# Second expert matrix read in 8 KB runs, and the sorted copy of the modulated rows made later by two engines

## The chip, the cores and the metric

The kernel runs on one core of one Trainium2 chip. The metric is the device time of one execution in microseconds (us). A core has a matrix engine (PE, with its weight loads as PEld), a vector engine (DVE), an activation engine (ACT), a general engine (POOL), and a queue engine (SP) that issues most of the transfers (DMA) between the main memory and the on-chip memory (SBUF). Matmuls write to a second memory, PSUM, in tiles of up to 512 columns per bank. About 0.2%, or 3.7 us, is what a measurement of this kernel can tell from no change.

## The reference

One layer on 512 tokens of width 1024, all in float32:

```python
h = modulate(rms_norm(x, g_mix[l]), sh_a, sc_a)
u = h @ w_in[l]
...
x = x + gt_a[:, None, :] * (merged @ w_o[l])
h = modulate(rms_norm(x, g_ffn[l]), sh_f, sc_f)
x = x + gt_f[:, None, :] * moe(h, w_router[l], b_router[l], w_mlp1[l], b_mlp1[l], w_mlp2[l], b_mlp2[l])
```

`merged` comes from a retention branch and from dilated attention with three head groups of four heads each; groups 1 and 2 take their keys with a stride. The second half is a mixture of 32 experts, four per token. One expert on its rows:

```python
u = xb @ w1[e] + b1[e]
glu = jnp.minimum(u[:, ::2], SWIGLU_LIMIT)
lin = jnp.clip(u[:, 1::2], -SWIGLU_LIMIT, SWIGLU_LIMIT)
a = glu * jax.nn.sigmoid(SWIGLU_ALPHA * glu) * (lin + 1.0)
return a @ w2[e] + b2[e]
```

`w1[e]` is 1024 x 2048, `w2[e]` is 1024 x 1024.

## The kernel before

**Precision.** Matmuls run on operands that are split in two parts, a rounded high part and the rest. ACT makes the high part (`w_hl` at L203 and L229, `w_hi` at L1045), DVE subtracts it from the raw tile for the low part (L204, L230, `w_lo` at L1051). DVE's instruction has both inputs in SBUF.

**Attention stage.** The modulated rows lie transposed in `hTh` and `hTl` (high and low part, 128 partitions x 8 chunks x 512 tokens). Groups 1 and 2 need the tokens sorted by their place modulo 4: ACT and DVE sort queries and keys when they copy them out of PSUM (`query`, L509; `key`, L515; group 0 unsorted at L507 and L517). For the values the rows themselves are the stationary operand, so a sorted copy `hpr` of `hTh` and `hTl` is made, 8 chunks each, by `reorder` on POOL (L438). It is read by the values of heads 1 to 3 (`unit_tok` with `hp`); head 0 reads the rows with a stride. `hpr` takes the buffer in which the bias table `pbt` lay.

For each head the order is: `scores` (PE L527 for groups 1 and 2, L535 for group 0; DVE adds the bias at L529 and L539, ACT takes the exponential at L544), a round trip of the softmax sums through main memory, issued by POOL (`st` at L545 and L546, `so` at L548 and L549), then the next head's query products, `merge` (DVE L554 to L567, which reads `so`), and `values` (transposes L584, products L595, sum L608, split L609 and L610). Then come a product for the modulation row (`ada_row_pe`, PE L273, DVE L275, store by POOL L278) and the next head's keys. `retire` splits the next weight tile whenever one has been used. In head 0 the 16 copies of `reorder` are issued between the query products. This part is in an order written by hand: each engine runs its instructions in the order of the code.

**Experts.** `tiles` lists 384 tiles of 1 MB: for each expert eight A tiles (128 rows of `w1`) and four B tiles (256 rows of `w2`), in the order A of expert e, then B of expert e - 1. Experts are sorted by load. Large ones ("L") have 96 slots and three matmul passes (high x high, low weights, low rows), small ones ("S") have 64 slots, and both parts of the rows stand side by side as one stationary operand, so two passes do. The kinds are `"LLLL" + "LS" * 14`. The tiles go through a ring of nine slots. SP loads a tile when DVE has made the low part of the tile nine places ahead; ACT works four tiles ahead of PE (`prep_hi`), DVE three (`prep_lo`). The first expert matrix comes with 2048 numbers (8 KB) per partition and tile. For the second one two rows of 1024 numbers, 128 rows apart, make up a partition's part:

```python
SP.dma_start(w.rearrange("p (k n) -> p k n", k=2),
             w2[0, at].rearrange("o (k p) n -> p (o k) n", p=P)[:, 2 * k:2 * k + 2])
```

**Around the activation.** `u` is one PSUM buffer of four banks. When an expert's A tiles are done, ACT writes the sigmoid `sg` (`open_gates`, L1200), DVE writes `av` (`linear`, L1205) and multiplies it in place (`times_glu`, L1209); these read every second column of `u`, and then the next expert's bias matmul (L1140) may write `u`. Later DVE multiplies `av` by `sg` (`times_gate`, L1212), PE transposes `av` in two halves of four chunks (`turn`, L1178), and ACT and DVE write the parts of `at` (`turn_copy`, L1122 and L1123). That is done in the A tiles 2 and 3 of the following expert, for the last expert ahead of its first B tile. B tile k then uses chunks 2k and 2k + 1 of `at` (L1369 for large, L1376 for small experts). For a large expert the sigmoid stands on ACT ahead of the last copy of the next expert's turned rows, `x`.

Of the kernel before, what the change touches and what calls it, by code (L numbers as in the profile page):

```python
# [12 lines left out]
F32R = mybir.dt.float32r  # L13
# [3 lines left out]
AF = mybir.ActivationFunctionType  # L17
# [97 lines left out]
def body(tc, a, out):  # L115
# [318 lines left out]
    def reorder(i, kcs):  # L434
        src = (hTh, hTl)[i]
        for kc in kcs:
            o, x = hp[i][:, kc].rearrange("p (t a) -> p t a", t=4), src[:, kc].bitcast(F32).rearrange("p (a t) -> p t a", t=4)
            G.tensor_copy(o, x)  # L438
    s1 = ExitStack()
    p1c = s1.enter_context(tc.tile_pool(name="p1c", bufs=1, side="right", reuse_waits="tile"))  # L440
    p1w = s1.enter_context(tc.tile_pool(name="p1w", bufs=2, side="right", reuse_waits="tile"))
# [176 lines left out]
    for h in range(4):  # L618
# [9 lines left out]
            unit_tok(parts["v0", 0], None, v0f, (0,))  # L628
            bias_flip(bf, range(4))
        s, st, so = scores(h, qT, kT)  # L630
        if h == 0:
            hpr = p2c.tile([P, 2, KC, S], F32R, name="hpr", tag="hp")
            hp = [hpr[:, 0], hpr[:, 1]]
        ada = ada_row_sum(h)
        if h == 0:
            unit_tok(parts["v0", 0], None, v0f, (1,))
# [9 lines left out]
        if h < 3:  # L646
            qT = []
            for g in range(3):
                qT.append(query(g, unit(None, hTh, hTl, parts=parts[AQ, g, h + 1])))
                retire(1)  # L650
                if h == 0:
                    for i in range(2):
                        reorder(i, range(3 * g, min(3 * g + 3, KC)))
                if g == 1:
                    merge(s, st, so)
            last = (AK, 1, h + 1)
        else:
            rq0 = unit_open("ps")
            unit_part(rq0, parts[RQ, 0], hTh, hTl, range(KC))
            merge(s, st, so)  # L660
            last = (RK, 0)
# [3 lines left out]
            kT = {1: key(1, pf)}  # L665
        retire(1)
        ada_row_pe(h, ada)
        if h < 3:
            for g in (2, 0):
                kT[g] = key(g, unit(None, hTh, hTl, parts=parts[AK, g, h + 1]))  # L670
                retire(1)
    s1.close()


# [200 lines left out]
    def load(i, pool, tag):  # L875
        kind, e, k = tiles[i]
        w = pool.tile([P, 2048], F32, name="w_moe", tag=tag)
        if kind == "A" and k == 0 and e > 1:
            which[e] = nc.values_load(sorted_i[0:1, e:e + 1], engines=[mybir.EngineType.SP], min_val=0, max_val=E - 1)
        at = ds(which[e], 1) if e > 1 else slice(e, e + 1)  # L880
        if kind == "A":
            SP.dma_start(w, w1[0, at].rearrange("o (k p) n -> p (o k) n", p=P)[:, k])
        else:
            SP.dma_start(w.rearrange("p (k n) -> p k n", k=2),
                         w2[0, at].rearrange("o (k p) n -> p (o k) n", p=P)[:, 2 * k:2 * k + 2])
        loaded[i] = w

    ring = [(wr, "wr")] * NRA + [(hl, "hl")] * NRC
# [304 lines left out]
    def fold(ps, low):  # L1193
        for j in range(ps.shape[1]):
            PE.matmul(ps[:SMALL, j], shift[SMALL:], low[SMALL:, j], start=False, stop=True, skip_group_check=True)

    def open_gates(u):
        n = u.shape[0]
        sg = m2.tile([CAP, 4, 256], F32, name="sg", bufs=1)[:n]
        A.activation(sg, u[:, :, ::2], AF.Sigmoid, scale=1.702)  # L1200
        return sg

    def linear(u):
        av = m2.tile([CAP, 4, 256], F32, name="av", bufs=1)[:u.shape[0]]
        V.tensor_scalar(av, u[:, :, 1::2], 8.0, -6.0, op0=OP.min, op1=OP.max)  # L1205
        return av

    def times_glu(u, av):
        V.scalar_tensor_tensor(av, u[:, :, ::2], 7.0, av, op0=OP.min, op1=OP.mult)  # L1209

    def times_gate(sg, av):
        V.scalar_tensor_tensor(av, sg, top7[:av.shape[0], 1:2], av, op0=OP.min, op1=OP.mult)  # L1212
# [107 lines left out]
    for i, (kind, e, k) in enumerate(tiles):  # L1320
# [33 lines left out]
        else:  # L1354
# [8 lines left out]
            if KIND[e] == "L":  # L1363
                ah, al = AT[e]
                for s_, m_ in ((ah, hi), (ah, lo), (al, hi)):
                    for c in range(2):
                        for n in range(2):
                            col = c * 1024 + n * 512
                            PE.matmul(Y[e][:CAP, n], s_[:, 2 * k + c], m_[:, col:col + 512], start=False,  # L1369
                                      stop=(k == 3 and s_ is al and c == 1))  # L1370
            else:
                for m_ in (hi, lo):
                    for c in range(2):
                        for n in range(2):
                            col = c * 1024 + n * 512
                            PE.matmul(Y[e][:, n], AT[e][2][:, 2 * k + c], m_[:, col:col + 512],  # L1376
                                      start=(k == 0 and c == 0 and m_ is hi), stop=False, skip_group_check=True)
                        if k == 0 and c == 0 and m_ is hi:
                            for n in range(2):
                                bias_mm(Y[e][:SMALL, n], e, 4 + n, False)  # L1380
# [62 lines left out]
    with tc.For_i(0, extra) as it:  # L1443
# [34 lines left out]
            PE.matmul(y[:, n], ones_r[0:1, :CAP], bb2[:, n * 512:(n + 1) * 512], start=True, stop=False)  # L1478
        for k in range(4):
            w = wc.tile([P, 2, D], F32, name="w_x2", tag="lo")  # L1480
            SP.dma_start(w, w2[0, ds(ev, 1)].rearrange("o (k p) n -> p (o k) n", p=P)[:, 2 * k:2 * k + 2])
            for c in range(2):
                for n in range(2):
                    PE.matmul(y[:, n], aT[:, 2 * k + c], w[:, c, n * 512:(n + 1) * 512], start=False,
                              stop=(k == 3 and c == 1))
        finish(y, gate_, idx)

# [50 lines left out]
```

## Time and profile before

| | us |
|---|---|
| median of 3 runs | 1853.34 (1851.53 to 1855.56) |
| the profiled execution | 1853.22 |
| its span, first to last instruction | 1851.4 |
| PE busy | 1750.5 (95%) |
| DVE busy | 1457.3 (79%) |
| ACT busy | 1094.7 (59%) |
| POOL busy | 349.7 (19%) |

The busy time is summed over the whole span, and the stages differ: up to about 620 us the projections, attention and retention, to about 720 us the output product and the router, to about 1800 us the experts, then the final norm. A row of the timeline has the start, the duration, the engine, the line, the operation, its operands (partitions x elements) and, in brackets, how long the engine was idle before and what ended that. Matmuls overlap, so the duration of one is longer than the step from one to the next.

### The profile page before, as it was taken

How to read it: one execution, taken by the hardware profiler on the slowest of the kernel's cores; microseconds unless marked ns; L12 is line 12 of the kernel's file. 1: busy time of each engine (PE TensorE's matmuls, PEld its weight loads, DVE VectorE, ACT ScalarE, POOL GpSimd, SP SyncE). 2: the span in 40 equal slices, each digit the busy share in tenths (PEclk: the TensorE clock that was granted, in tenths of full speed). 3: DMA queues.
4: the chain of work that ended last, by engine and by line, in shares of the span. 5: the costliest groups of instructions: out<-in, count | busy, mean ns of one | idle time of the engine just before them, and what ended most of it. 6: DMA issues, size and time to landing. Idle time of an engine off the chain costs nothing.

```text
span 1851.4 us, 23571 instructions
## 1 busy us (share of the span) xinstructions
PE 1750.5 (95%) x8625; PEld 1329.4 (72%) x8625; DVE 1457.3 (79%) x1490; ACT 1094.7 (59%) x1064; POOL 349.7 (19%) x220
## 2 busy tenths in 40 slices
PE   5988999999999998999999999999999999999982
PEld 4877888888778876677766776776676677677661
DVE  7555535657564558799989999999999999999994
ACT  5232233222222324677878977987887887898781
POOL 2031001100110111023631221211212112122111
PEclk8998999999999997999999999999999999999996
DMA  9523423633565555799999999999999999999993
GB/s 314 158 69 92 114 72 89 208 91 95 162 171 148 178 231 204 275 369 374 373 367 389 405 388 397 397 396 401 385 408 399 388 404 394 385 405 390 397 356 115
DMA packets 207910, 525.49 MB, mean 284 GB/s; under 512 B 12102, under 2 KB 127222, under 8 KB 174896
## 3 DMA queue, kind: packets, MB, share of 16 engines
q1 hardware_dynamic: 197744, 494.99, 71.5%
q0 software_dynamic: 10048, 28.98, 6.3%
q8 instruction: 69, 1.13, 0.3%
q14 instruction: 49, 0.40, 0.1%
HBM read 503.67 MB, written 20.25 MB: 283 GB/s over the span
## 4 chain that ended last, share of the span: by engine, by line
PE 74%; DVE 12%; DMA 7%; issue 4%; ACT 3%; SPq 0%; DVEq 0%; POOL 0%; ACTq 0%; POOLq 0%
PE u L1344 22%; DVE w_lo L1051 6%; PE pp L213 6%; PE pp L215 6%; PE pp L214 6%; PE y L1369 5%; PE u L1349 5%; PE y L1376 5%; DMA w_moe<-in_w_mlp 4%; DMA s_acc<-ys,idx 2%; PE pp L247 2%; PE pp L245 2%; PE pp L246 2%; PE pt L1178 2%; PE u L1140 2%
## 5 line engine op out<-in xcount | busy, mean ns | idle before, releaser
L1051 DVE TENSOR_TENSOR w_lo<-w_moe,w_hi 128x2048 fp32r<-128x2048 f32 x384 | 862.7, 2277 | 11.1 <-ACT w_hi L1045 5.7
L1045 ACT ACTIVATE w_hi<-w_moe 128x2048 fp32r<-128x2048 f32 x384 | 728.6, 1914 | 166.5 <-PE u L1344 103.9
L1344 PE MATMUL u<-w_hi,x 128*96 128x512 f32 x1152 | 313.2, 402 | 0.1
L1169 POOL DMA_INDIRECT xg<-s_h,idx x31 | 145.9, 4705 | 669.7 <-ACT gate L1165 345.8
L1344 PEld LDWEIGHTS u<-w_hi,x 128*96 128x96 f32 x1152 | 182.4, 163 | 75.2 <-issue 0.3
L213 PE MATMUL pp<-hTh,w_hl 128*128 128x512 f32 x400 | 160.4, 401 | 0.0
L1344 PE MATMUL u<-w_lo,x 128*96 128x512 f32 x576 | 158.8, 398 | 1.2 <-DVE w_lo L1051 1.2
L214 PE MATMUL pp<-hTl,w_hl 128*128 128x512 f32 x400 | 156.6, 391 | 0.0
L215 PE MATMUL pp<-hTh,w_hl 128*128 128x512 f32 x400 | 156.5, 391 | 0.0
L1369 PE MATMUL y<-w_hi,at 128*96 128x512 f32 x576 | 153.1, 398 | 0.0
L204 DVE TENSOR_TENSOR w_hl<-w_raw,w_hl 128x1024 fp32r<-128x1024 f32 (+1 forms) x66 | 87.5, 1338 | 76.8 <-ACT w_hl L203 76.8
L1349 PE MATMUL u<-w_lo,x 128*128 128x512 f32 x448 | 125.7, 402 | 3.7 <-DVE w_lo L1051 2.6
L1349 PE MATMUL u<-w_hi,x 128*128 128x512 f32 x448 | 128.9, 409 | 0.0
L1219 POOL DMA_INDIRECT s_acc<-ys,idx x32 | 97.3, 3040 | 164.7 <-ACT ys L1218 149.3
L1344 PEld LDWEIGHTS u<-w_lo,x 128*96 128x96 f32 x576 | 94.4, 164 | 42.8 <-DVE w_lo L1051 1.6
L1369 PEld LDWEIGHTS y<-w_hi,at 128*96 128x96 f32 x576 | 92.1, 162 | 38.7 <-issue 0.4
L203 ACT ACTIVATE w_hl<-w_raw 128x1024 fp32r<-128x1024 f32 (+1 forms) x66 | 65.2, 1001 | 70.8 <-PE pp L215 54.1
L1349 PEld LDWEIGHTS u<-w_lo,x 128*128 128x128 f32 x448 | 82.0, 188 | 34.3 <-DVE w_lo L1051 15.8
L1349 PEld LDWEIGHTS u<-w_hi,x 128*128 128x128 f32 x448 | 79.1, 188 | 19.9 <-issue 5.4
L213 PEld LDWEIGHTS pp<-hTh,w_hl 128*128 128x128 f32 x400 | 75.5, 189 | 17.9 <-issue 3.1
L215 PEld LDWEIGHTS pp<-hTh,w_hl 128*128 128x128 f32 x400 | 75.4, 188 | 16.2
L214 PEld LDWEIGHTS pp<-hTl,w_hl 128*128 128x128 f32 x400 | 75.5, 189 | 14.6
(342 smaller groups left out, 2699.2 us busy)
## 6 DMA issues: line engine op xcount, KB each, us to landing
w_moe<-in_w_mlp SPq DMA_DIRECT2D x384, 1024.0 KB, 12.9
w_raw<-in_w_in SPq DMA_DIRECT2D x76, 512.0 KB, 5.4
w_ada<-in_w_ada SPq DMA_DIRECT2D x24, 1024.0 KB, 7.1
w_raw<-in_w_ret_o SPq DMA_DIRECT2D x8, 512.0 KB, 4.7
w_o<-in_w_o SPq DMA_DIRECT2D x4, 1024.0 KB, 5.0
s_acc<-z POOLq DMA_DIRECT2D x5, 512.0 KB, 7.2
xin<-in_x SPq DMA_DIRECT2D x4, 512.0 KB, 6.6
w_raw<-in_w_att_o SPq DMA_DIRECT2D x8, 256.0 KB, 6.4
```

The source lines that it names most:

```text
L204: eng.tensor_tensor(lo[:, :kc], raw, hi[:, :kc].bitcast(F32), op=OP.subtract)
L213: PE.matmul(ps, hi[:, k], mh[:, k], start=(k == 0), stop=False)
L214: PE.matmul(ps, hi[:, k], ml[:, k], start=False, stop=False)
L215: PE.matmul(ps, lo[:, k], mh[:, k], start=False, stop=(k == kc - 1))
L1045: A.activation(his[i], loaded[i], AF.Copy)
L1051: V.tensor_tensor(los[i], loaded[i], his[i].bitcast(F32), op=OP.subtract)
L1169: G.indirect_dma_start(out=xg, out_offset=None, in_=xn2, in_offset=bass.IndirectOffsetOnAxis(ap=idx[:, :1], axis=0))
L1219: G.indirect_dma_start(out=acc, out_offset=bass.IndirectOffsetOnAxis(ap=idx[:, :1], axis=0), in_=ys, in_offset=None, compute_op=OP.add)
L1344: PE.matmul(U[e][:CAP, j], s_[:, k], m_[:, j * 512:(j + 1) * 512], start=False, stop=(k == KC - 1 and s_ is xl))
L1349: PE.matmul(U[e][:, j], X[e][2][:, k], m_[:, j * 512:(j + 1) * 512], start=(k == 0 and m_ is hi), stop=False, skip_group_check=True)
L1369: PE.matmul(Y[e][:CAP, n], s_[:, 2 * k + c], m_[:, col:col + 512], start=False, stop=(k == 3 and s_ is al and c == 1))
L1376: PE.matmul(Y[e][:, n], AT[e][2][:, 2 * k + c], m_[:, col:col + 512], start=(k == 0 and c == 0 and m_ is hi), stop=False, skip_group_check ...
```

## The change

For the second expert matrix each partition reads 2048 consecutive numbers, that is rows 2p and 2p + 1 of a tile's 256, where it read rows p and p + 128. The stationary chunks must hold the same rows: chunk 4c + k has to hold the rows 256k + 2p + c. This order is made when `sg` and `av` are written: `by_row` is the sorted view of an SBUF tile, `pairs` the view of `u` that goes with it. Element 2m + c is written to place 512c + m.

The sorted copy of the modulated rows is made after head 0's `values` and the modulation row: the low part by POOL in eight copies, the high part by ACT in two groups of four among the next head's key products.

```diff
+            if i:
+                G.tensor_copy(o, x)
+            else:
+                A.activation(o, x, AF.Copy)
...
-                if h == 0:
-                    for i in range(2):
-                        reorder(i, range(3 * g, min(3 * g + 3, KC)))
...
         ada_row_pe(h, ada)
+        if h == 0:
+            hpr = p2c.tile([P, 2, KC, S], F32R, name="hpr", tag="hp")
+            hp = [hpr[:, 0], hpr[:, 1]]
+            reorder(1, range(KC))
         if h < 3:
-            for g in (2, 0):
+            for i, g in enumerate((2, 0)):
                 kT[g] = key(g, unit(None, hTh, hTl, parts=parts[AK, g, h + 1]))
                 retire(1)
+                if h == 0:
+                    reorder(0, range(4 * i, 4 * i + 4))
...
-            SP.dma_start(w.rearrange("p (k n) -> p k n", k=2),
-                         w2[0, at].rearrange("o (k p) n -> p (o k) n", p=P)[:, 2 * k:2 * k + 2])
+            SP.dma_start(w, w2[0, at].rearrange("o (k p c) n -> p (o k) (c n)", p=P, c=2)[:, k])
...
+    def by_row(t):
+        return t.rearrange("p j i -> p (j i)").rearrange("p (c m) -> p m c", c=2)
+
+    def pairs(u, i):
+        return u.rearrange("p j i -> p (j i)")[:, i::2].rearrange("p (m c) -> p m c", c=2)
+
-        A.activation(sg, u[:, :, ::2], AF.Sigmoid, scale=1.702)
+        A.activation(by_row(sg), pairs(u, 0), AF.Sigmoid, scale=1.702)
...
-        V.tensor_scalar(av, u[:, :, 1::2], 8.0, -6.0, op0=OP.min, op1=OP.max)
+        V.tensor_scalar(by_row(av), pairs(u, 1), 8.0, -6.0, op0=OP.min, op1=OP.max)
...
-        V.scalar_tensor_tensor(av, u[:, :, ::2], 7.0, av, op0=OP.min, op1=OP.mult)
+        V.scalar_tensor_tensor(by_row(av), pairs(u, 0), 7.0, by_row(av), op0=OP.min, op1=OP.mult)
...
-                            PE.matmul(Y[e][:CAP, n], s_[:, 2 * k + c], m_[:, col:col + 512], start=False,
+                            PE.matmul(Y[e][:CAP, n], s_[:, 4 * c + k], m_[:, col:col + 512], start=False,
```

The same new index stands in the small experts' matmul, and the new load and index in the loop for overflowing experts.

On POOL, from head 0's stores of the softmax sums to those of head 1, before the change (L438 is `reorder`, L259 and L278 load and store the modulation row, L522 clears a part of `s` for the next `scores`):

```order
L545 DMA s_sta<-st 128x4x2
L546 DMA s_stb<-st 128x8
L548 DMA so<-s_stb 128x4x2
L549 DMA so<-s_sta 128x8
L259 DMA brow<-in_b_ada 1x16x16
L438 CAST hpr<-hTh 128x512 x3
L438 CAST hpr<-hTl 128x512 x3
...
L278 DMA s_mod<-brow 16x1x16
L522 MEMSET s 128x128
```

And after it (line numbers of the changed kernel):

```order
L548 DMA s_sta<-st 128x4x2
L549 DMA s_stb<-st 128x8
L551 DMA so<-s_stb 128x4x2
L552 DMA so<-s_sta 128x8
L259 DMA brow<-in_b_ada 1x16x16
L278 DMA s_mod<-brow 16x1x16
L439 CAST hpr<-hTl 128x512 x8
L525 MEMSET s 128x128
```

The copies went from the place ahead of the store of the modulation row to the place behind it, and eight of the sixteen left this engine.

On ACT, the end of head 0's `values` to the exponentials of head 1, after the change (L441 is `reorder`, L203 and L229 are the high parts of weight tiles, L612 is the high part of the attention output, L547 the exponential, L590 and L610 copy out of PSUM):

```order
L590 ACTIVATE pT<-pt 128x384
L610 ACTIVATE ao<-po 128x512
L612 ACTIVATE atH<-ao 128x512
L229 ACTIVATE w_hl<-w_raw 128x4x128 x4
L203 ACTIVATE w_hl<-w_raw 128x1024
L441 ACTIVATE hpr<-hTh 128x512 x4
L203 ACTIVATE w_hl<-w_raw 128x1024
L441 ACTIVATE hpr<-hTh 128x512 x4
L547 ACTIVATE s,st<-s,st 128x256 x8
```

Before the change the two splits L203 stood next to each other, and there were no copies into `hpr` on ACT.

On DVE, around the activation of a large expert in the changed kernel (L1053 is `w_lo`, L1125 the low part of turned rows, L1213 `linear`, L1217 `times_glu`, L1220 `times_gate`):

```order
L1053 TENSOR_TENSOR w_lo<-w_moe,w_hi 128x2048
L1125 TENSOR_TENSOR x<-pt,x 128x4x64
L1053 TENSOR_TENSOR w_lo<-w_moe,w_hi 128x2048
L1213 TENSOR_SCALAR av<-u 96x512x2
L1217 SCALAR_TENSOR_TENSOR av<-u,av 96x512x2
L1053 TENSOR_TENSOR w_lo<-w_moe,w_hi 128x2048 x2
```

The order is that of before; the two `av` instructions have the form 96x512x2 where they had 96x1024.

## Rows read from the trace of the kernel before

**Rows 1.** Busy time by stage; columns: stretch, length, PE, PEld, DVE, ACT, POOL, clock, DMA.

```profile
1000.00:1250.00 250.00, 248.60 (x1183) 176.09 (x1181) 240.07 (x150) 206.91 (x165) 52.75 (x15) 1.00 1.02 395
```

**Rows 2.** Chain of waits through one pair of experts; columns: start, length, what.

```profile
1000.20 5.54 PE u L1344 x24
...
1046.80 0.04 DVEq L1051
...
1064.16 1.23 DVE av L1209
...
1065.53 1.13 PE u L1140 x4
```

**Rows 3.** Timeline of another pair, ACT and DVE around the activation.

```profile
1224.14 1.02 ACT L1200 ACTIVATE sg<-u 96x1024 f32<-96x1024 f32 x1 [1.39 <-PE u L1344]
1225.07 0.37 ACT L1122 ACTIVATE x<-pt 128x256 fp32r<-128x256 f32 x1
1225.47 0.43 DVE L1123 TENSOR_TENSOR x<-pt,x 128x256 fp32r<-128x256 f32 x1 [2.48 <-ACT x L1122]
...
1263.65 1.22 DVE L1209 SCALAR_TENSOR_TENSOR av<-u,av 64x1024 f32<-64x1024 f32 x1
```

**Rows 4.** Waits in 1000 to 1750 us; columns: total us, times, longest.

```profile
ACT w_hi L1045 <- DMA w_moe<-in_w_mlp: 8.2, 16, 1.7
```

**Rows 5.** Waits of the queue engine in 1000 to 1750 us.

```profile
SPq L882 <- DVE w_lo L1051: 267.4, 149, 3.0
```

**Rows 6.** Instructions by form in 1000 to 1750 us; after the bar: busy us, mean ns.

```profile
L1209 DVE SCALAR_TENSOR_TENSOR av<-u,av 96x1024 f32<-96x1024 f32 x11 | 13.4, 1221 | 0.4
L1205 DVE TENSOR_SCALAR av<-u 96x1024 f32<-96x1024 f32 x11 | 13.4, 1214 | 0.0
...
L1200 ACT ACTIVATE sg<-u 96x1024 f32<-96x1024 f32 x11 | 11.2, 1021 | 15.1 <-PE u L1344 15.1
```

**Rows 7.** DVE by form in 80 to 330 us: a sum in steps, a difference in plain order.

```profile
L608 DVE TENSOR_TENSOR ao<-ao,po 128x512 f32<-128x512 f32 x4 | 4.4, 1091 | 19.8 <-PE po L595 19.8
...
L610 DVE TENSOR_TENSOR atL<-ao,atH 128x512 fp32r<-128x512 f32 x4 | 2.8, 692 | 2.8 <-ACT atH L609 2.8
```

**Rows 8.** DVE by form in 560 to 760 us: copies that write in a row, in steps.

```profile
L945 DVE CAST selb<-sel 128x128 bf16<-128x128 f32 x4 | 0.9, 228 | 0.1
...
L963 DVE CAST aux<-rg 128x120 bf16<-128x120 f32 x1 | 0.4, 439 | 0.0
```

**Rows 9.** Timeline of head 0 for POOL, DVE and PE, engine by engine.

```profile
125.96 3.15 POOL L438 CAST hpr<-hTh 128x512 fp32r<-128x512 f32 x3
...
140.39 2.10 POOL L438 CAST hpr<-hTl 128x512 fp32r<-128x512 f32 x2
...
130.09 13.48 DVE L204 TENSOR_TENSOR w_hl<-w_raw,w_hl 128x1024 fp32r<-128x1024 f32 x1 [4.21 <-ACT w_hl L203]
...
133.53 0.39 PE L215 MATMUL pp<-hTh,w_hl 128*128 128x512 f32 x1
145.54 1.17 PE L584 MATMUL pt<-misc,s 128*128 128x128 f32 x4 [11.62 <-DVE s L567]
```

**Rows 10.** Chain of waits, heads 0 and 1: first transposes and modulation product.

```profile
157.76 0.52 PE pb L273 x2
...
200.58 0.44 PE pt L584 x4
...
211.14 0.52 PE pb L273 x2
```

**Rows 11.** Timeline behind head 0's values for POOL, DVE and PE, engine by engine.

```profile
164.46 0.22 POOL L522 MEMSET s<- 128x128 f32 x1
...
165.10 1.23 DVE L204 TENSOR_TENSOR w_hl<-w_raw,w_hl 128x1024 fp32r<-128x1024 f32 x1 [0.41 <-ACT w_hl L203]
...
169.45 0.69 DVE L517 COPY k<-pp 128x512 f32<-128x512 f32 x1 [3.12 <-PE pp L215]
...
171.04 1.69 PE L535 MATMUL sc<-k,q 128*128 128x128 f32 x8
```

More of the change, by code (lines that the diff above doesn't have):

```diff
@@ L437, in reorder @@
             o, x = hp[i][:, kc].rearrange("p (t a) -> p t a", t=4), src[:, kc].bitcast(F32).rearrange("p (a t) -> p t a", t=4)
-            G.tensor_copy(o, x)
+            if i:
+                G.tensor_copy(o, x)
+            else:
+                A.activation(o, x, AF.Copy)
     s1 = ExitStack()
@@ L630, in body @@
         s, st, so = scores(h, qT, kT)
-        if h == 0:
-            hpr = p2c.tile([P, 2, KC, S], F32R, name="hpr", tag="hp")
-            hp = [hpr[:, 0], hpr[:, 1]]
         ada = ada_row_sum(h)
@@ L650, in body @@
                 retire(1)
-                if h == 0:
-                    for i in range(2):
-                        reorder(i, range(3 * g, min(3 * g + 3, KC)))
                 if g == 1:
@@ L1375, in body @@
                             col = c * 1024 + n * 512
-                            PE.matmul(Y[e][:, n], AT[e][2][:, 2 * k + c], m_[:, col:col + 512],
+                            PE.matmul(Y[e][:, n], AT[e][2][:, 4 * c + k], m_[:, col:col + 512],
                                       start=(k == 0 and c == 0 and m_ is hi), stop=False, skip_group_check=True)
@@ L1480, in body @@
             w = wc.tile([P, 2, D], F32, name="w_x2", tag="lo")
-            SP.dma_start(w, w2[0, ds(ev, 1)].rearrange("o (k p) n -> p (o k) n", p=P)[:, 2 * k:2 * k + 2])
+            SP.dma_start(w, w2[0, ds(ev, 1)].rearrange("o (k p c) n -> p (o k) c n", p=P, c=2)[:, k])
             for c in range(2):
                 for n in range(2):
-                    PE.matmul(y[:, n], aT[:, 2 * k + c], w[:, c, n * 512:(n + 1) * 512], start=False,
+                    PE.matmul(y[:, n], aT[:, 4 * c + k], w[:, c, n * 512:(n + 1) * 512], start=False,
                               stop=(k == 3 and c == 1))
```

## The prediction

> **What bounds the kernel now.** I read the table by stage first, then the chain of waits inside one stage, then the waits, and last the single rows. From about 740 us to 1800 us the kernel streams 32 experts, and there all three resources are nearly full: in 1000 to 1250 us PE is busy 248.60 of 250 us, DVE 240.07, and the DMA engines read 1.02 [rows 1]. Such shares name no bound, so the chain decides. The experts come as four large ones (L, three matmul passes) and then 14 pairs of a large and a small one (S, two passes). One pair is 66.4 us: the chain enters the A tiles of a large expert at 1000.20 and the next large one's bias matmul at 1065.53 [rows 2]. Up to 1046.80 the chain is PE's; from there it is DVE's, ending with `linear` (L1205) and `times_glu` (L1209), which read the one PSUM buffer `u` and so free it for PE's next bias matmul (L1140). PE starts 0.14 us after L1209's end at 1065.39.
>
> The stretch of PE and that of DVE are tied together. When PE ends the A tiles of a large expert, ACT makes the sigmoid (L1200, 1224.14), then copies the transposed rows of the next expert (1225.07), and DVE, idle for 2.48 us, goes on at 1225.47 [rows 3]. From there DVE has no gap of this kind until L1209 at 1263.65 has freed `u` for the next large expert, at 1264.87. In that run lie both L1205/L1209 couples of the pair, the large expert's early and the small one's at the end. So a pair is: PE's A tiles of the large expert (about 25 us), the ACT sigmoid and one copy (1.4 us), then 39.4 us of DVE. Whatever is added to one of the four DVE instructions, or to the large expert's sigmoid, is added to the pair.
>
> DMA has no such place. SP issues its loads when DVE has released a slot (267.4 us of waits behind `w_lo` in 750 us) [rows 5], and ACT, which uses the tiles first, waited for a load only 8.2 us in 750, 16 times [rows 4]. ACT is idle at other times, and PE and DVE were not found waiting behind these.
>
> Earlier there is one large hole: in head 0 PE is idle 11.62 us before the transposes at 145.54 [rows 9]. DVE is the cause, and POOL behind it: the split of a weight tile (L204) that begins at 130.09 lasts 13.48 us, where its like lasts 1.23, and POOL makes its 16 copies into `hpr` from 125.96 to 142.49. L204 has two SBUF inputs; it ended at 143.57, 1.08 us after POOL's last copy. `merge` stands behind it on DVE, and its last step lets PE go on.
>
> **The change part by part.** *Loads in runs of 8 KB.* The same 1 MB per tile, the same queue and slots, 128 loads in the other shape. The 8.2 us in 750, some 11 in the 1050 us of this stage, bound what it can give, and nothing on the chain waits for it: I take 0, between a gain of 11 us and nothing. If this cover went, ACT would wait for tiles, and `w_lo` behind it.
>
> *PE's side.* Chunk 4c + k of `at` in place of 2k + c. Both halves of the turned rows are made in the A tiles of the following expert, ahead of the B tiles, and for the last expert both before its first B tile: no new wait, 0.
>
> *The price of the other row order.* Rows 2p and 2p+1 of a run of 8 KB lie in one partition, so the activations must be sorted, and the change does it where they are written: `sg` and `av` are written with neighbours 512 elements (2 KB) apart, and `times_glu` also reads `av` so. Counts per expert: one ACT instruction (L1200, now 1.02 us) and two DVE instructions (L1205 1.21, L1209 1.22) [rows 6]. At 1024 elements these run at about one element per cycle now, so a gain is excluded. What a jump at each element costs, no row shows for this distance. Nearest is L608, which reads and writes SBUF in steps of four elements, in place, as L1209 will: 1.091 us against 0.692 for L610 of the same size with plain rows, so 0.40 us per 512 elements [rows 7], 0.80 per 1024. L1209 is of this kind: 0.80. L1205 only writes in jumps: between 0 and 0.80. That a stepping write alone costs is seen in L963, 439 ns for 120 elements written in steps, against 228 for 128 in a row [rows 8]; that is 1.76 ns per element and 1.8 us per 1024, the upper end for either instruction. I take 0.70 for L1205, near L608. For ACT no row has an SBUF operand in steps; between 0 and 0.80, I take 0.40.
>
> The Trainium skill (Vector Engine (DVE) Microarchitecture Reference, "Measured stream behaviour on trn2") says that a DVE port runs at full rate only when consecutive elements come in adjacent pairs, and gives 1.71 ns per column for a destination that hops 4 KiB at every element and 1.98 with all streams hopping, against 1.054. As an estimate from that page L1205 would take 0.67 us more and L1209 0.95, and the forecast would be 3 us higher. No run here shows it at 2 KB.
>
> The sum for this part: per pair 2 x (0.70 + 0.80) + 0.40 = 3.4 us; the small expert's sigmoid isn't on the run. 14 pairs give 47.6 us. In the first four experts, all large, PE has 12 matmuls per tile of 0.231 us (5.54 us for 24 [rows 2]), 2.77 us against a small expert's 1.85, for the same work of DVE; there PE is the longer one, and I count nothing.
>
> *The sorted copy moved.* Removed: POOL's 16 copies in head 0, so L204 takes its 1.23 us and ends near 131.3; the load of `so` that `merge` reads is issued by POOL ahead of the first copy, 5 us before; from L204's end to the transposes it takes 2.0 us (143.57 to 145.54), so they are due near 133.3, when PE is still at its last matmuls (the last starts at 133.53). The 11.62 us go. With them goes PE's slow start behind the hole: from the transposes to the `ada` product 145.54 to 157.76 is 12.22 us in head 0, 200.58 to 211.14 is 10.56 in head 1 [rows 10], 1.66 us more. Gain: 13.28 us.
>
> Added: POOL makes eight copies behind the store of the `ada` row of head 0. Today a memset of `s` stands there at 164.46 [rows 11]; the copies take half of 16.53 us, so till 172.73 (times before the shift). DVE's next L204 comes at 165.10 and waits as the one in head 0 did, to 1.08 us after POOL: 173.81. Behind it stands the copy of the first group's keys (L517), from 169.45 to 170.14 today, then to 174.50; PE's scores of that group (L535) started at 171.04 and wait till 174.55. That is 3.5 us of PE, plus between 0 and 1.66 for a slow start behind a shorter hole, I take 0.5. Behind the copies on POOL stand the memset and, later, the stores of `st`; DVE writes `s` only from about 175.7, behind another split of 1.23 us, so the memset is in time. ACT's eight copies, each between 0.51 (half of L1200) [rows 6] and POOL's 1.05 [rows 9], go four behind the split of which L204 at 165.10 is DVE's half, and four behind the next one at 169.45: done by 174.8 at the latest, and the product that reads `hpr` now starts near 176. Net gain of this part: 13.28 - 3.5 - 0.5 = 9.3 us.
>
> The Trainium skill (SBUF — State Buffer, "Who interferes with whom") says that DVE with two SBUF inputs and a reading POOL instruction exclude each other for the length of one instruction, whoever starts first. By that L204 would get in after one copy (1.05 us), L517 would not be late, the 3.5 us would not arise and the forecast would be 4 us lower; the row of 13.48 us, behind twelve copies, speaks against it.
>
> **Forecast.** The profiled execution took 1853.2 us (span 1851.4 and 1.8 around it), the median of the three runs is 1853.3, so nothing has to be scaled. 1853.2 - 9.3 + 47.6 = 1891.5 us.
>
> **The rivals.** *Jumps of 2 KB cost DVE and ACT nothing.* For it: L1205 and L1209 read PSUM in steps of two today at one element per cycle [rows 6], so steps alone need not cost. Against it: L608 and L963. Then the part in the experts is 0 and the time 1843.9, faster. It decides from 9.3 / 14 = 0.66 us per pair, about 0.16 us for each of the four DVE instructions: below that the kernel is not slower. *They cost a part*, only one of the two instructions or a third of L608's price: 14 x 0.5 to 14 x 1.7, so 1851 to 1868. *They cost as in L963*, 1.8 us each on DVE and ACT: 14 x (4 x 1.8 + 1.8) = 126, so 1970. *The loads of 8 KB pay*: the 11 us of waits come back, 1880; inside the range. *POOL lets DVE in between two copies*: L204 waits one copy of 1.05 us at most, PE's 4.0 us are not lost, 1887.5; against it stands L204's 13.48 us, so 0.1 of the forecast's chance.
>
> **How the numbers follow.** Forecast, with the terms of L1205 between 0.4 and 0.8, L1209 between 0.6 and 1.0 and ACT between 0 and 0.8, 1872 to 1905: chance 0.70. Free: 0.15. A part: 0.09. As L963 or in between: 0.06. The range 1850 to 1920 leaves out the free case and the dearest one. About 0.2%, 3.7 us, is what a measurement of this kernel can tell from no change. Faster by more: 0.16, nearly all from the free case; within: 0.03; slower: 0.81.
>
> **What would show it.** Right: `av` on DVE near 1.9 and 2.0 us in place of 1.21 and 1.22, a pair of experts near 69.8 us in place of 66.4, PE waiting at L1140 for `av`, and ACT's waits for loads gone without effect; in head 0 no L204 of 13 us and no hole before the transposes, and in head 1 one L204 of about 8.7 us with PE waiting some 3.5 us before L535. Wrong: `av` at 1.2 us, or `av` longer and the pair still 66.4 us (then DVE had slack that I don't see), or a changed rate of the loads that moves the pair.

## The result, and the profile after

| | before | after |
|---|---|---|
| median, four runs each on the same chip, us | 1853.19 (1851.53 to 1855.56) | 1912.69 (1910.41 to 1913.47) |
| after over before, 95% interval | | 1.0317 (1.0303 to 1.0330) |
| span of the profiled execution, us | 1851.4 | 1910.3 |

The change makes the kernel 59.5 us slower; the forecast was 38.3 us slower. The sign was right, and so was the mechanism in the stage of the experts; the size was too small by 21 us.

The stage of the experts comes first. Its busy times by stretch, in the order of [rows 1]:

```profile
1000.00:1250.00 250.00, 238.79 (x1104) 164.09 (x1104) 233.02 (x141) 196.09 (x153) 82.23 (x14) 0.99 0.98 372
```

PE was busy 248.60 of 250 us and is now busy 238.79. DVE didn't fill the place: it went from 240.07 to 233.02, because fewer experts pass in the same time. So PE waits, and the chain of waits shows for what. This is one pair of experts, to be read against [rows 2] (start, length, what):

```profile
1000.17 1.14 PE u L1142 x4
1001.31 5.55 PE u L1352 x24
...
1030.68 1.96 DVE av L1213
1032.65 2.15 DVE av L1217
1034.94 1.17 PE u L1357 x4
...
1066.67 1.96 DVE av L1213
1068.66 2.07 DVE av L1217
1070.86 1.99 PE u L1142 x4
```

The pair takes 70.69 us (1000.17 to 1070.86), where it took 66.47 (999.06 to 1065.53). Both couples of `linear` (L1213) and `times_glu` (L1217) now lie on the chain, with 1.96 to 2.15 us each. The two forms of each in 1000 to 1750 us (behind the bar busy us and mean ns), to be read against [rows 6]:

```profile
L1217 DVE SCALAR_TENSOR_TENSOR av<-u,av 96x1024 f32<-96x1024 f32 x11 | 23.5, 2140 | 0.4
L1217 DVE SCALAR_TENSOR_TENSOR av<-u,av 64x1024 f32<-64x1024 f32 x11 | 22.8, 2069 | 0.4
L1213 DVE TENSOR_SCALAR av<-u 96x1024 f32<-96x1024 f32 x11 | 22.3, 2029 | 0.0
L1208 ACT ACTIVATE sg<-u 96x1024 f32<-96x1024 f32 x11 | 22.3, 2025 | 15.1 <-PE u L1352 15.1
```

`linear` went from 1.21 to 2.03 us, `times_glu` from 1.22 to 2.10 (mean of the two forms), the sigmoid of the large experts from 1.02 to 2.03. The waits in the same 750 us (total us, times, longest):

```profile
PE u L1142 <- DVE av L1217: 21.8, 11, 2.0
PE u L1357 <- DVE av L1217: 7.1, 10, 0.7
```

PE waits 2.0 us for `av` ahead of each large expert and 0.7 ahead of each small one. Before, PE was idle for 0.26 us at that place in the pair of [rows 2].

Attention is the other place. POOL, DVE and PE around heads 0 and 1, against [rows 9] and [rows 11]:

```profile
149.89 8.43 POOL L439 CAST hpr<-hTl 128x512 fp32r<-128x512 f32 x8
...
128.84 1.23 DVE L204 TENSOR_TENSOR w_hl<-w_raw,w_hl 128x1024 fp32r<-128x1024 f32 x1 [4.21 <-ACT w_hl L203]
150.53 8.87 DVE L204 TENSOR_TENSOR w_hl<-w_raw,w_hl 128x1024 fp32r<-128x1024 f32 x1 [0.40 <-ACT w_hl L203]
...
132.50 0.60 PE L587 MATMUL pt<-misc,s 128*128 128x128 f32 x4
...
160.15 3.32 PE L538 MATMUL sc<-k,q 128*128 128x128 f32 x8 [3.52 <-DVE k L520]
```

The split at 128.84 takes 1.23 us and the transposes follow at 132.50 without a hole. In head 1 the split at 150.53 waits behind POOL's eight copies and takes 8.87 us, and PE waits 3.52 us for the key copy behind it.

The 58.9 us between the two spans, cut at the bias matmul on `u` of the experts named (from the timeline):

| stretch | before | after | difference |
|---|---|---|---|
| start to expert 0 | 710.47 | 702.63 | -7.84 |
| expert 0 to 4 | 152.77 | 156.35 | +3.58 |
| 4 to 5 | 38.12 | 38.02 | -0.10 |
| the 13 steps from a small to a large expert | 413.16 | 451.58 | +38.42 |
| the 13 steps from a large to a small one | 453.87 | 476.30 | +22.43 |
| expert 31 to the end | 83.01 | 85.42 | +2.41 |

### The profile page after: what moved, and what is told of

It is laid out like the page before. It is cut to its first block, busy times and chain, and to the rows that moved or that the text cites. A ratio compares the mean times of both kernels' runs of the same rounds, so it can differ in the third digit from the quotient of the medians.

```text
span 1910.3 us, 23571 instructions
## 1 busy us (share of the span) xinstructions
PE 1775.6 (93%) x8625; PEld 1326.6 (69%) x8625; DVE 1503.5 (79%) x1490; ACT 1132.9 (59%) x1072; POOL 457.5 (24%) x212
## 2 busy tenths in 40 slices
DMA packets 191526, 525.49 MB, mean 275 GB/s; under 512 B 12102, under 2 KB 127222, under 8 KB 142128
## 4 chain that ended last, share of the span: by engine, by line
PE 65%; DVE 27%; issue 4%; DMA 2%; ACT 1%; DVEq 0%; SPq 0%; POOL 0%; POOLq 0%; ACTq 0%
PE u L1352 22%; DVE w_lo L1053 16%; PE pp L213 6%; PE pp L215 6%; PE pp L214 6%; PE u L1357 5%; DVE av L1217 3%; DVE av L1213 3%; PE y L1377 2%; PE pp L247 2%; PE pp L245 2%; PE pp L246 2%; PE u L1142 2%; PE pt L1180 1%; PE y L1384 1%
## 5 line engine op out<-in xcount | busy, mean ns | idle before, releaser
L1053 DVE TENSOR_TENSOR w_lo<-w_moe,w_hi 128x2048 fp32r<-128x2048 f32 x384 | 862.2, 2277 | 5.7 <-issue 2.7
L1227 POOL DMA_INDIRECT s_acc<-ys,idx x32 | 303.1, 9473 | 233.8 <-ACT ys L1226 217.8
L1352 PE MATMUL u<-w_hi,x 128*96 128x512 f32 x1152 | 318.6, 407 | 0.0
L1171 POOL DMA_INDIRECT xg<-s_h,idx x31 | 57.6, 1858 | 546.8 <-PE y L1384 264.0
L204 DVE TENSOR_TENSOR w_hl<-w_raw,w_hl 128x1024 fp32r<-128x1024 f32 (+1 forms) x66 | 82.9, 1268 | 78.0 <-ACT w_hl L203 78.0
L1357 PE MATMUL u<-w_lo,x 128*128 128x512 f32 x448 | 130.8, 413 | 11.9 <-DVE w_lo L1053 10.2
L1357 PEld LDWEIGHTS u<-w_lo,x 128*128 128x128 f32 x448 | 77.3, 188 | 60.2 <-DVE w_lo L1053 46.7
L203 ACT ACTIVATE w_hl<-w_raw 128x1024 fp32r<-128x1024 f32 (+1 forms) x66 | 65.2, 1002 | 66.7 <-PE pp L215 45.2
```

What stands on the lines that cost most here:

```text
L203: A.activation(hi[:, :kc], raw, AF.Copy)
L204: eng.tensor_tensor(lo[:, :kc], raw, hi[:, :kc].bitcast(F32), op=OP.subtract)
L1053: V.tensor_tensor(los[i], loaded[i], his[i].bitcast(F32), op=OP.subtract)
L1171: G.indirect_dma_start(out=xg, out_offset=None, in_=xn2, in_offset=bass.IndirectOffsetOnAxis(ap=idx[:, :1], axis=0))
L1227: G.indirect_dma_start(out=acc, out_offset=bass.IndirectOffsetOnAxis(ap=idx[:, :1], axis=0), in_=ys, in_offset=None, compute_op=OP.add)
L1352: PE.matmul(U[e][:CAP, j], s_[:, k], m_[:, j * 512:(j + 1) * 512], start=False, stop=(k == KC - 1 and s_ is xl))
```

## The experiments

Each run was timed beside the kernel before on its own chip, which gave medians of 1852.8 to 1853.4 us.

**The two parts apart.** The second part alone takes over the new `reorder` and its calls and leaves loads and activations as before:

```diff
-                if h == 0:
-                    for i in range(2):
-                        reorder(i, range(3 * g, min(3 * g + 3, KC)))
...
+            reorder(1, range(KC))
...
+                    reorder(0, range(4 * i, 4 * i + 4))
```

> The kernel before with the second part alone: the sorted copy moved behind head 0's values and shared by POOL and ACT; loads and activations as before. Theory of the prediction: the hole of 11.62 us in head 0 and the slow start behind it go, and 3.5 to 4 us come back as a wait of the group-0 scores in head 1, so 9.3 us less than before, 1844. The trace of the changed kernel stands 7.8 us ahead at the first expert, of which 1.3 us lie ahead of the first instruction, so 1844 to 1847. Rival: the time of the attention stage is taken up again by a wait for loads at the start of the experts, then 1853.

Measured: 1843.43 us, ratio 0.9952 (0.9935 to 0.9968), 9.9 us less. The first part alone, with the loads, the index and the sorted writes:

> The kernel before with the first part alone: loads of 8 KB runs, activations written sorted, the sorted copy of the rows where it was. Theory: the two parts add up, so the changed kernel's 1912.7 plus the 7 to 9 us that the other part gives: 1920 to 1922. The step from a small to a large expert is 3.3 us longer than before, and from a large to a small one 0.9 or 2.5 us. Rival: part of the loss is a collision of the two parts (an earlier start that the loads then have to catch up with), then 1910 to 1914.

Measured: 1922.03 us, ratio 1.0363 (1.0345 to 1.0380), 68.7 us more. The parts add up: 68.7 - 9.9 = 58.8, and the change gave 59.5. The rival of a collision falls. (In the profiled executions a lower clock behind a wait, told below, came in nine places with the first part alone and in seven with the whole change, 3.2 us apart; closer than that the sum can't be read.)

**What the loads are worth.** The loads and the index, with plain `sg` and `av`:

```diff
+            SP.dma_start(w, w2[0, at].rearrange("o (k p c) n -> p (o k) (c n)", p=P, c=2)[:, k])
...
+                            PE.matmul(Y[e][:CAP, n], s_[:, 4 * c + k], m_[:, col:col + 512], start=False,
```

> The kernel before with the loads of 8 KB runs and the new chunk index, and no sorting anywhere: the activations are left in plain order, so they meet the wrong rows of the second expert matrix; the work is otherwise that of before. It shows what the loads alone are worth. In the kernel with the sort at the transposes ACT waited for loads 3.8 us in the experts against 8.2, and none of the steps from a small to a large expert was longer than 31.75 us, where before three of thirteen were, by 3.8 us together. Theory: the loads give 3 to 5 us, 1849. Rival A, as predicted: 0, 1853. Rival B: they give the 11 us, 1842.

Measured: 1853.09 us, ratio 1.0000 (0.9990 to 1.0010). My theory here fell and the prediction's zero stands. ACT's waits for loads between 740 and 1770 us are

```profile
ACT w_hi L1044 <- DMA w_moe<-in_w_mlp: 8.2, 11, 2.1
```

and the kernel before has 8.2 us too, in 16 waits. The late steps that I had put down to the short runs occur here as well: 32.02, 32.44 and 35.74 us where 31.65 is the rule. They come at partly other experts in each run, and the loads' shape doesn't decide on them.

What makes such a step long shows in the chain of the kernel before, here through its step of 32.77 us (start, length, what):

```profile
1437.80 13.90 DMA w_moe<-in_w_mlp
...
1451.81 1.92 ACT w_hi L1045
1453.73 0.03 issue
1453.76 1.88 ACT low L1190
...
1455.68 1.14 PE u L1195 x4
```

`low` (L1190) is ACT's copy of the part of a small expert's products that PE then adds to the rest (L1195). In this step ACT waited 1.71 us for a tile, where in a step of 31.64 us (expert 19) it waited 0.46 for the tile of the same place; so `low` came late and PE waited 1.48 us for it. PE waits for `low` in four places between 740 and 1770 us in the kernel before, 3.7 us in total, and in four with the loads in the new shape, 4.0 us. So loads do reach the chain in a few places, which the prediction had left out, and longer runs don't cure it.

**Where the sort is made: on PE.** The activations are written in plain order, and the transposes read every second column:

```diff
+            part = rows[:, 2 * P * i + q:2 * P * (i + 1):2] if by_two else rows[:, c * P:(c + 1) * P]
+            PE.transpose(pt[:, i, :n], part, ident[:n, :n])
```

> The kernel before with the loads of 8 KB runs and the new index of the chunks, but the activations written in plain order; the sort is made where PE transposes them: each transpose reads 128 of 256 columns with step 2. The sorted copy of the rows stays where it was. Theory (the jumping writes alone cost the time): L1205 and L1209 are back at 1.21 us, the sigmoid at 1.02, a pair at 66.4 us, the time 1853, between 1850 (if the longer runs of the loads give a little) and 1856 (if PE pays for the stepping read of its stationary operand, 16 transposes per expert). Rival A: the loads of 8 KB themselves hold up the pair, then over 1870 with av at 1.21 us. Rival B: the loads pay by the 11 us of waits that ACT has for them: 1842.

Measured: 1859.04 us, ratio 1.0031 (1.0021 to 1.0040), 5.7 us more; `av` is back at 1.21 us. Rival A falls with it: the loads don't hold up the pair. The 5.7 us are PE's. The weight load of one transpose of a small expert's `av` in 1000 to 1750 us, first before, then here:

```profile
L1178 PEld LDWEIGHTS pt<-misc,av 64*128 64x128 f32 x96 | 7.8, 139 | 9.3 <-issue 8.9 <-DVE w_lo L1051 0.4
```

```profile
L1178 PEld LDWEIGHTS pt<-misc,av 64*128 64x128 f32 x92 | 12.7, 208 | 8.9 <-issue 8.9
```

That is 69 ns for each of eight transposes, 0.55 us. They lie in the A tiles of the large expert that follows, where PE is on the chain, and the step from a large to a small expert grew from 34.83 to 35.28. The transposes of a large expert's `av` lie in the other step and need as much more (207 ns against 141), but that step stayed at 31.65: DVE has no gap there. 13 x 0.45 = 5.9 us. Other steps of the two profiled executions differ too, by up to 2.7 us, some up and some down, so the match with 5.7 is not as close as it looks.

**Where the sort is made: while reading PSUM.** The same sorted `sg` and `av`, but the instructions walk through the SBUF tile in order and through `u` in steps of four. Only the order of the dimensions in the two views differs from the change:

```diff
-        return t.rearrange("p j i -> p (j i)").rearrange("p (c m) -> p m c", c=2)
+        return t.rearrange("p j i -> p (j i)").rearrange("p (c m) -> p c m", c=2)
...
-        return u.rearrange("p j i -> p (j i)")[:, i::2].rearrange("p (m c) -> p m c", c=2)
+        return u.rearrange("p j i -> p (j i)")[:, i::2].rearrange("p (m c) -> p c m", c=2)
```

> The kernel before with the loads of 8 KB runs, the new chunk index and the sorted sg and av, but each of the three instructions walks through the sorted tile in order and steps through u instead: SBUF written and read in plain rows, PSUM read in steps of four elements instead of two. Theory (jumps on the SBUF side cost, steps in PSUM don't): L1205 and L1209 at 1.21, the sigmoid at 1.02 us, and the time of the kernel with the loads alone, 1849 to 1851. Rival: a step of four in PSUM costs like one in SBUF, 0.8 us per 1024 elements: then the time of the first part alone, 1915 to 1922.

Measured: 1853.57 us, ratio 1.0001 (0.9991 to 1.0011). The three instructions in 1000 to 1750 us:

```profile
L1214 DVE SCALAR_TENSOR_TENSOR av<-u,av 96x1024 f32<-96x1024 f32 x11 | 13.4, 1220 | 0.4
L1210 DVE TENSOR_SCALAR av<-u 96x1024 f32<-96x1024 f32 x11 | 13.4, 1214 | 0.0
...
L1205 ACT ACTIVATE sg<-u 96x1024 f32<-96x1024 f32 x11 | 11.2, 1021 | 15.2 <-PE u L1349 15.2
```

They take as long as before. So the whole price of the first part is the jump on the SBUF side, and it was not needed: the same order of values comes at no cost from the step in PSUM.

The trace of the kernel before had this to show already. In attention, ACT's copies of queries at L509 and DVE's of keys at L515 sort while they step through PSUM by four elements and write SBUF in a row; L507 and L517 copy without sorting (80 to 330 us):

```profile
L507 ACT ACTIVATE q<-pp 128x512 f32<-128x512 f32 x6 | 3.6, 595 | 15.7 <-PE pp L215 15.7
L509 ACT ACTIVATE q<-pp 128x512 f32<-128x512 f32 x3 | 1.8, 599 | 7.5 <-PE pp L215 7.5
...
L517 DVE COPY k<-pp 128x512 f32<-128x512 f32 x3 | 2.1, 692 | 11.0 <-PE pp L215 11.0
L515 DVE COPY k<-pp 128x512 f32<-128x512 f32 x6 | 4.1, 687 | 1.0 <-PE pp L215 1.0
```

The sort costs neither engine anything there, so the cheap order of the dimensions could have been chosen from the trace.

**DVE's share and ACT's share.** Sorted writes for the sigmoid alone, and for `av` alone, each with the new loads:

```diff
-        A.activation(sg, u[:, :, ::2], AF.Sigmoid, scale=1.702)
+        A.activation(by_row(sg), pairs(u, 0), AF.Sigmoid, scale=1.702)
```

> The kernel before with the loads of 8 KB runs and the new index, where only the sigmoid sg is written in jumps and av in plain order: the two factors don't match then, so the activation is computed in part wrongly; the work is the same. Theory: the sigmoid is 1.0 us longer, that of the large expert lies in the pair's run, and the step from a large to a small expert grows by 0.95 us, fourteen times, 13 us over the kernel with the loads alone: 1862 to 1863. The step from a small to a large one stays at 31.65. Rival: the 0.95 us belongs to DVE's longer instructions, and ACT has room for its longer one: 1849 to 1850.

```diff
-        V.tensor_scalar(av, u[:, :, 1::2], 8.0, -6.0, op0=OP.min, op1=OP.max)
+        V.tensor_scalar(by_row(av), pairs(u, 1), 8.0, -6.0, op0=OP.min, op1=OP.max)
...
-        V.scalar_tensor_tensor(av, u[:, :, ::2], 7.0, av, op0=OP.min, op1=OP.mult)
+        V.scalar_tensor_tensor(by_row(av), pairs(u, 0), 7.0, by_row(av), op0=OP.min, op1=OP.mult)
```

> The first part of the change with av written in jumps (both DVE instructions) and the sigmoid sg in plain order: the two factors don't match then, so the activation is computed in part wrongly; the work is the same. The counterpart of the kernel with the jumping sigmoid alone, which is 7.5 us slower than before with 0.95 us more per pair. Theory (the terms of a pair add up): 2 x (0.82 + 0.89) = 3.4 us per pair, 48 us, plus up to eight steps that are 1.6 us longer by the lower clock, so 1901 to 1914, and a pair 0.95 us shorter than in the first part alone. Rival: the longer sigmoid hides behind the longer DVE instructions, then 1922 like the first part alone.

Measured: 1860.76 us (ratio 1.0046, 1.0029 to 1.0063) and 1908.73 us (1.0298, 1.0281 to 1.0315). The steps between the bias matmuls of experts 8 (large), 9 (small) and 10 (large), from the timelines:

| kernel | 8 to 9 | 9 to 10 | the pair |
|---|---|---|---|
| before | 34.83 | 31.64 | 66.47 |
| sigmoid in jumps | 34.86 | 32.61 | 67.47 |
| `av` in jumps | 34.84 | 34.93 | 69.77 |
| both (the changed kernel) | 35.78 | 34.91 | 70.69 |
| both (the first part alone) | 37.36 | 34.94 | 72.30 |

The sigmoid adds 1.00 us to a pair, `av` 3.30, both 4.22: the terms add, as the sum in the prediction had it. The sigmoid shows in the second step where it jumps alone, and in the first where `av` jumps as well. My expectation had the wrong step; I take it to be a matter of where PE meets the wait, which no run tests. Where only `av` jumps, nine of the thirteen steps from a large to a small expert are 1.6 us longer (36.45), of which the next experiment tells more. The sigmoid's share of the total is only 7.5 us. Twelve of the 13 steps from small to large are 0.96 us longer, 11.5 us, but their sum grew by 7.6 (413.16 to 420.75). Before, three of them were longer than their like (32.77, 33.72 and 32.24 against 31.64), 3.8 us together, and here none is. These are steps with the waits for `low` told above; in that of 33.72 us the granted clock also fell behind the wait of 0.88 us (0.74 in 1525 to 1530 us). With the sigmoid in jumps ACT waits for no load between 740 and 1770 us, nor does it in the changed kernel, and in none of these steps does PE wait for `low`. So a slower pair leaves the late loads more time, and part of its price comes back.

**The lower clock behind the wait.** In the table the first part alone has a step of 37.36 where the changed kernel has 35.78. Both values occur in both kernels: in the changed one, from expert 6 on, seven of the thirteen such steps take about 37.36 us and six 35.8 (the expectation below says eight, which is one too many). Ten matmuls that nobody reads were put in the place of the wait:

```diff
+                    if e and KIND[e - 1] == "S":
+                        warm = psC.tile([P, 4, CAP], F32, name="warm", tag="pt", bufs=2)
+                        for _ in range(10):
+                            PE.matmul(warm[:CAP].rearrange("p a b -> p (a b)"), sel[:, 0, e:e + 1].to_broadcast([P, CAP]),
+                                      btile[:, :4 * CAP], start=True, stop=True)
```

> The changed kernel with ten matmuls of 384 columns, whose result nobody reads, ahead of the bias matmul of each large expert that follows a small one, where PE waits some 2 us for av. In the changed kernel eight of the steps from a large to a small expert are 37.36 us and six 35.8; in the long ones the granted clock is 0.68 to 0.72 in the 5 us behind the wait. Theory: the wait lets the clock fall, and work in its place keeps it up; all steps become 35.8, 8 x 1.6 = 12.7 us less than the changed kernel, 1900. Rival: the long steps have another cause (the bias matmul itself, or the load of its weights), then 1912 to 1913, or more if the added matmuls run into the bias matmul's time.

Measured: 1899.88 us, ratio to before 1.0254 (1.0237 to 1.0271), 12.8 us less than the changed kernel. All thirteen steps are 35.77 to 35.83 us. In the changed kernel, the 5 us behind the bias matmul of experts 10 and 12, with the granted clock in the last but two column:

```profile
1071.00:1076.00 5.00, 5.00 (x16) 3.38 (x17) 5.00 (x3) 0.85 (x1) 3.87 (x1) 0.68 1.02 351
1143.30:1148.30 5.00, 5.00 (x22) 3.46 (x22) 5.00 (x3) 1.99 (x2) 3.94 (x1) 1.00 1.03 342
```

Both came behind a wait of 2.0 us, and PE began 16 matmuls in the one stretch and 22 in the other; 0.68 is a mix of the two levels, 1.2 and 2.4 GHz. With the matmuls in the wait:

```profile
1067.58 1.89 PE L1349 MATMUL warm<-btile,selrow 128*96 128x384 f32 x10
...
1069.80 1.13 PE L1142 MATMUL u<-btile,selrow 128*96 128x512 f32 x4 [0.33 <-DVE av L1217]
```

```profile
1069.80:1074.80 5.00, 5.00 (x22) 3.55 (x23) 5.00 (x3) 1.97 (x2) 3.83 (x1) 1.00 1.03 341
```

The matmuls fill 1.89 of the 2 us, the steps to a large expert stay within 0.1 us of what they were, and the clock stays up. So about 11 us (7 x 1.58), of the 59.5, are a second price of the wait.

**No copy on POOL.** To test whether DVE waits for POOL's copies at all, all sixteen were given to ACT, in the order of before otherwise:

```diff
-            G.tensor_copy(o, x)
+            A.activation(o, x, AF.Copy)
...
+                if h == 0 and g == 0:
+                    reorder(0, range(4))
...
+            if h == 0 and r == 1:
+                reorder(0, range(4, KC))
...
+                if h == 0:
+                    reorder(1, range(4 * i, 4 * i + 4))
```

> The kernel before with all 16 sorted copies on ACT and none on POOL: four behind the first query group of head 1, four behind the first transposes, four and four behind key products of head 1; loads and activations as before. Theory (DVE waits until POOL has no copy left, and PE behind it): no weight split of 8 or 13 us on DVE, neither hole, 13.3 us less than before: 1840, or up to 1844 if ACT's 1.1 us per copy put off one of its splits of weight tiles by 4.4 us. Rival: ACT is late for the exponentials or for the weight splits of head 1 by all of its 17.7 us, then 1850 or more.

Measured: 1837.55 us, ratio 0.9914 (0.9898 to 0.9931), 15.8 us less than before. DVE's split in head 1 and ACT's first exponential there: first with the second part alone, then with all copies on ACT:

```profile
150.86 8.85 DVE L204 TENSOR_TENSOR w_hl<-w_raw,w_hl 128x1024 fp32r<-128x1024 f32 x1 [0.40 <-ACT w_hl L203]
...
166.26 0.51 ACT L547 ACTIVATE s<-s,st 128x256 f32<-128x256 f32 x1 [5.94 <-DVE st L545]
```

```profile
150.77 1.23 DVE L204 TENSOR_TENSOR w_hl<-w_raw,w_hl 128x1024 fp32r<-128x1024 f32 x1 [0.40 <-ACT w_hl L203]
...
162.26 0.51 ACT L544 ACTIVATE s<-s,st 128x256 f32<-128x256 f32 x1 [1.91 <-DVE st L542]
```

Before, the exponential comes at 176.58. Set against the splits at 120.56 (before), 119.63 and 119.55, which lie ahead of the first difference, the second part brings it forward by 9.39 us and the copies on ACT by 13.31. The time of the whole kernel fell by 15.8 us, with an interval of 12.8 to 18.9 that takes in the 13.3. ACT's copies take 1.03 us each (4.13 for four), and PE is busy for all of the 60 us from 120 to 180.

**Put together.** The change with the views in the other order, and the copies on ACT with loads and views:

> The changed kernel with both parts, where the three activation instructions walk through the sorted tile in order and through u in steps of four. Theory: the jumps cost nothing then, the loads neither give nor cost, and what is left is the moved copy: 1843 to 1845, like the second part alone. Rival: the late loads seen in some steps weigh more once the first experts start earlier, then 1850.

> All sixteen sorted copies on ACT, none on POOL, together with the loads of 8 KB and the sort made in the order of reading. Theory: the time of the copies on ACT alone, 1837 to 1839, since the loads are worth nothing. Rival: with the longer runs the late loads are fewer, then 1834 to 1836.

Measured: 1843.89 us (ratio 0.9947, 0.9931 to 0.9964) and 1839.11 (0.9926, 0.9910 to 0.9943). The first is the second part of the change by itself, as it should be. The second is not told apart from the copies on ACT alone, 1837.55. So the lowest time of the study needs neither the longer loads nor a sort: all copies on ACT, 0.9% faster than before.

## Why the prediction came out as it did

The 1912.7 us lie inside the range of 1850 to 1920, but above the 1872 to 1905 that the prediction's own terms allowed and to which it gave 0.70; they fell where it had given 0.06. The structure held. That the outer range took the result in is in part luck: terms that were too small or missing came to 25.4 us, and 4.8 us came back from a side that was not in the sum.

*The structure of a pair*: right. Each term added to the four `av` instructions or to the large expert's sigmoid was added to the pair, to within 0.2 us (by the lengths 2 x (0.82 + 0.88) = 3.40 for `av`, measured 3.30; the sigmoid 1.00 and 1.00).

*The price of the jumps*: too small. L1205 +0.82 against 0.70, L1209 +0.88 against 0.80, L1200 +1.00 against 0.40. A pair is 4.22 us longer where I had 3.4. The large miss is ACT: with no row I took the middle between nothing and L608's price, and it was above that end. For DVE the row of L608 [rows 7], 0.80 per 1024 elements, was a good guide, though its steps are of 16 bytes and these jumps of 2 KB. The Trainium skill (Vector Engine (DVE) Microarchitecture Reference, "Measured stream behaviour on trn2") gives 1.71 and 1.98 ns per column against 1.054 for jumps of 4 KB; by it, as an estimate, an expert pays 0.67 + 0.95 = 1.62 us on DVE, and the trace has 1.70, near it, though more evenly divided.

*Nothing in the first four experts*: wrong, by 3.6 us. Expert 1 waits 6.2 us for `av` where it waited 3.7:

```profile
PE u L1142 <- DVE av L1217: 6.9, 2, 6.2
```

This row is of 700 to 900 us. The chain into expert 1 in the changed kernel has the three instructions one behind the other:

```profile
739.34 1.94 ACT sg L1208
...
741.30 1.98 DVE av L1213
...
743.29 2.06 DVE av L1217
...
745.49 0.71 PE u L1142
```

Before, they stand there with 1.03, 1.23 and 1.23 us, and PE waits 3.71 us. No B tiles come between expert 0's A tiles and expert 1, so PE has nothing to do meanwhile, and each of the three prices is paid in full: 2.5 of the 3.6 us. Where the rest comes from was not followed. My comparison of PE's tile with DVE's tile left out that the first expert has no such cover.

*The clock behind the new wait*: not in the sum at all, 11 us. I had priced the slow start of PE behind holes in attention and did not ask whether the new wait ahead of each large expert would bring the same.

*What comes back*: not in the sum either. The longer steps of before, 3.8 us from small to large (behind late loads) and 1.6 in the one from expert 6 to 7 (36.41 against 34.83; ACT waits 10.7 us there for a landing of `s_acc`, and not in the changed kernel), vanish in the slower rhythm; the last step, shorter before (34.20), takes 0.6 of it back.

*Loads and index*: 0 forecast, 0.0 measured (loads alone 1853.09, with the plain sort in PSUM 1853.57). The page of the changed kernel counts 191,526 packets where there were 207,910, and the time doesn't notice. The number was right and its reason only in the main: that nothing on the chain waits for a load does not hold in the three longer steps, and the longer runs left such steps as they were.

*The moved copy*: forecast -9.3; -9.9 by time in the part alone, -9.39 in its trace. The stall ahead of the group-0 scores was forecast as 3.5 us and is 3.52. In the profiled run of the changed kernel it cost somewhat more, since the clock was 0.50 from 160 to 166 us and the eight matmuls of L538 took 3.32 us, where the part alone had 1.00 and 1.76; the range of 0 to 1.66 us given for that term covers it. The rival in which POOL lets DVE in between copies falls: a split of 8.87 us behind eight copies, 1.23 with none. The Trainium skill (SBUF — State Buffer, "Who interferes with whom") says that the one that starts first holds the other off for its whole instruction; here DVE was held off for more than one, and its split ended 1.08 us behind the last of POOL's copies.

Together, against the span: the 14 pairs cost 42.2 us in the steps from small to large (2.75 + 12 x 3.29), 12.35 in the others (13 x 0.95) and 2.41 behind the last expert, 57.0 where I had 47.6. So the prices missed by 9.4, the clock by 11.1, the first experts by 3.5; 4.8 came back; and the moved copy gave 7.84 up to expert 0, 1.4 less than forecast. That is 20.6 us, the difference between 58.9 and 38.3.

## What to carry to other kernels

When values must be put in another order on their way from PSUM to SBUF, let the SBUF side run in order and step through PSUM: the order of the dimensions in the two views decides between 1.21 and 2.03 us for the same 1024 elements. A wait of 2 us on PE costs more than itself where the clock falls behind it; when PE can't be fed, matmuls that nobody reads may be worth their place. And a better shape of the loads was worth nothing here, not even in the few steps that a late load made longer: the table of waits says who waits for a transfer, but not that its shape is the reason.

## What the runs showed that was not expected

- ACT pays more than DVE for a jump at each element in SBUF: 1.02 to 2.03 us for 1024 elements, DVE 1.21 to 2.03.
- Steps in PSUM cost neither engine anything: 1.21 and 1.02 us for 1024 elements in steps of two and of four, 0.60 and 0.69 us for 512 in steps of four and in a row.
- PE loads its stationary operand of 128 columns in 208 ns instead of 139 when the columns are read in steps of two.
- The same wait of 2.0 us lowered the granted clock behind it in seven places of thirteen; what decides in which is open.
- POOL's issue of the indirect add `s_acc` takes 9.88 us on average in the changed kernel and 1.99 before, the same in the kernel with `av` alone in jumps (9.47), and not with the sigmoid alone (1.79). No wait for it shows in the changed kernel, and its cause was not looked into.
